# Group-wise modulation of the first norm in a diffusion layer, with the context rows prepared last

## The chip, the core and the metric

The kernel runs on one core of a Trainium2 chip. Its time is the device time of one launch in microseconds (us). "Before" is the median of three runs. The engines are TensorE (matmuls, PE in the profile; its weight loads are PEld), VectorE (DVE), ScalarE (ACT), GpSimd (POOL) and SyncE (SP), which issues nearly all DMA transfers here.

## What is computed

One layer of a diffusion transformer over 1024 latent tokens of 1024 features (x) with 256 context tokens (ctx), all in float32. What matters here is its beginning:

```python
sh1, sc1, g1, sh2, sc2, g2 = split(silu(c) @ w_mod + b_mod, 6)        # for the latents
csh1, csc1, ...            = split(silu(c_ctx) @ w_mod + b_mod, 6)    # for the context
h_lat = rms_norm(x, norm1_g) * (1 + sc1) + sh1
h_ctx = rms_norm(ctx, norm1_g) * (1 + csc1) + csh1
p_lat, p_ctx = h_lat @ w_in, h_ctx @ w_in      # columns: seven blocks of 512
```

`w_mod` is 1024 x 6144; the first norm uses its first 2048 columns, 1024 of shift and 1024 of scale. `w_in` is 1024 x 3584. Behind this stand retention and differential attention, an output projection and a gated MLP with a convolution; the change doesn't touch them.

## The kernel before

Features lie in 8 blocks of 128 (`KD` = 8, index `d` or `k`), latent tokens in 8 tiles of 128 (t = 0 to 7), context tokens in 2. A float32 product is made of three fast passes: each operand is split into a high part and a low part, and `passes` (L126) adds high x high, high x low and low x high (L129, L130, L131). The activations are kept transposed, features on partitions, as `hT[0]` (high) and `hT[1]` (low), each in two halves of 512 tokens; the context's are `cT`. A slice of `w_in` (two feature blocks of 512 columns, 512 KB, tile `raw`) is loaded and split into `whi` and `wlo` by `split_slice` (L181), four slices a block of columns; each call of `more` prepares one.

The first stage has these parts:

- `mod_part(i, q)` (L509) multiplies the two silu vectors (`cz`, padded to 32 columns for four strips of the array) with half of the rows of the i-th piece of `w_mod`, 512 columns wide. It loads two `wt` tiles of 512 KB, which share five buffers, and adds into the PSUM tile `pr`. Each call is four float32 matmuls, which the profile shows as eight. Between its loads the first four calls issue the load of one row tile of x (`xs`).
- `mod_columns(i)` (L522) copies `pr` to SBUF (`rw`, ScalarE), turns it into columns with four small matmuls (`pm`, eight in the profile) and adds the bias into `mcol` (VectorE; for a scale also the norm's gain).
- The four pieces come in the order scale of feature blocks 0 to 3, shift of 0 to 3, scale of 4 to 7, shift of 4 to 7; `lay_out` puts them so.
- `normalize` (L535) makes a row tile's sum of squares on ScalarE (`sq`), the reciprocal root on VectorE and GpSimd (`rsqrt`, L113) and the scaled rows on VectorE (L539).
- `modulate` (L541) does one feature block of up to four row tiles: TensorE transposes them into PSUM (`pt`, L545), ScalarE writes the high part (L548), VectorE the full value (`tmp`, L550), and VectorE or GpSimd, by turns, the low part (L552). `first_latents(half)` (L560) calls it for four blocks.
- `part_products(t, k)` (L564) adds feature block k's three passes into row tile t's PSUM tile `pn`, for column block 6 of `w_in`.

The order in the source (L590 to L627): pieces 0 and 1 with the first four row tiles, `first_latents(0)`, products of k = 0 to 3 for t = 0 to 3 with pieces 2 and 3 in between, `first_latents(1)`, products of k = 4 to 7 for t = 0 to 3. Beside these last run the steps of `other_rows` (L568): normalise the two context tiles and row tiles 4 to 7, modulate the context's eight blocks, then the latents' other eight. `beside(g, rate)` (L378) sets such a generator, and `tick` (L372), called after each product of three passes, takes `rate` steps of it on average; setting a new one first runs off the old one. Then come the context products of block 6 (L626), outside this scope row tiles 4 to 7 (L641), and the next stage, `transposed` with column block 5 (L644), whose PSUM tile is `pl`.

The source doesn't fix the engines' order. The framework schedules by its own estimates, with the source's order as priority, and so an engine's sequence in the trace can differ: the first product stands at 28.38 us on TensorE, and transposes of `first_latents(0)` that the source has ahead of it stand at 31.86 us. Within an engine's queue, and within SP's queue of DMA issues, the order is then fixed, and an instruction that waits holds those behind it.

## Time and profile before

| | us |
|---|---|
| median of three runs (lowest, highest) | 1414.38 (1412.52, 1414.53) |
| span of the profiled execution, first to last instruction | 1413.6 |
| first product `pn` starts | 28.38 |
| first `pl` starts (next stage) | 107.51 |
| TensorE busy | 1372.1 |
| VectorE / ScalarE / GpSimd busy | 991.1 / 729.1 / 286.1 |

The profile is of one execution, whose own time is known as its span, 1413.6 us. All times in the trace are counted from the span's start. Matmuls are pipelined and their ends are modelled, so two that follow each other overlap in the rows: what a matmul costs is read from one start to the next, not from its length. "Granted clock" is the share of full speed that TensorE's throttle gave. A wait is put down to what came last before the instruction started.

### The profile page before, as it was taken

Reading aid. Unit: us, or ns where it says so; the run is one execution under the profiler, and the core shown is the slowest. Engines: PE = TensorE matmul, PEld = TensorE weight load, DVE = VectorE, ACT = ScalarE, POOL = GpSimd, SP = SyncE. Lnnn points to the kernel's source line nnn. Section 1 sums busy time; section 2 is a strip of 40 time slices with the busy share of each in tenths; the row PEclk is TensorE's granted clock in tenths of the full one; section 3 lists DMA queues with packets and bytes.
Section 4 is the critical chain, followed back from the end, with each engine's and each line's share of the span. In section 5 each row is a group of like instructions: output and inputs, shape, how many; then the busy total and the mean of one; then the engine's idle time right before and its main releaser. Section 6 shows DMA issues by size and latency. Waiting matters only on the chain.

```text
span 1413.6 us, 19193 instructions
## 1 busy us (share of the span) xinstructions
PE 1372.1 (97%) x6924; PEld 1141.8 (81%) x6924; DVE 991.1 (70%) x1433; ACT 729.1 (52%) x1386; POOL 286.1 (20%) x321
## 2 busy tenths in 40 slices
PE   6999999999999999999999999999999999999996
PEld 2588888888888799998888778888888888888885
DVE  3464965334586798896357888877788777898457
ACT  3453312333565689997126645554455555455533
POOL 1220000000556133411201232233322220000001
PEclk8999999999999999999999999999999999999999
DMA  8645886365474796631421223223233226953224
GB/s 305 228 135 179 280 293 202 116 201 183 149 246 159 196 220 153 128 79 62 163 82 60 90 105 112 92 109 112 97 112 112 81 84 221 393 180 105 90 97 178
DMA packets 96662, 218.79 MB, mean 155 GB/s; under 512 B 9204, under 2 KB 31220, under 8 KB 96056
## 3 DMA queue, kind: packets, MB, share of 16 engines
q1 hardware_dynamic: 88408, 192.67, 39.3%
q0 software_dynamic: 8160, 24.91, 7.8%
q8 instruction: 54, 0.88, 0.2%
q14 instruction: 40, 0.33, 0.1%
HBM read 160.13 MB, written 57.41 MB: 154 GB/s over the span
## 4 chain that ended last, share of the span: by engine, by line
PE 81%; DMA 5%; issue 5%; DVE 4%; POOL 2%; ACT 2%; SPq 0%; POOLq 0%; DVEq 0%; ACTq 0%
PE pA L748 5%; PE pv L780 5%; PE chain L129 5%; PE chain L130 5%; PE chain L131 5%; PE c L131 4%; PE c L129 4%; PE c L130 4%; PE pn L130 3%; PE pn L129 3%; PE pn L131 3%; PE pl L129 3%; PE pl L131 3%; PE pl L130 3%; PE third L129 2%
## 5 line engine op out<-in xcount | busy, mean ns | idle before, releaser
L129 PE MATMUL chain<-T,whi 128*128 128x512 f32 x264 | 104.2, 395 | 4.7 <-ACT ua L1161 3.9
L129 PE MATMUL pl<-hT,whi 128*128 128x512 f32 x256 | 106.2, 415 | 0.0
L130 PE MATMUL chain<-T,whi 128*128 128x512 f32 x264 | 104.1, 394 | 0.0
L131 PE MATMUL chain<-T,wlo 128*128 128x512 f32 x264 | 103.9, 394 | 0.0
L131 PE MATMUL pl<-hT,wlo 128*128 128x512 f32 x256 | 100.2, 391 | 0.0
L130 PE MATMUL pl<-hT,whi 128*128 128x512 f32 x256 | 100.0, 391 | 0.0
L751 DVE TENSOR_REDUCE mt<-pA 128x1 f32<-128x1280 f32 x64 | 95.3, 1490 | 3.6 <-PE pA L748 2.1
L131 PE MATMUL c<-whi,ghl 128*128 128x512 f32 x232 | 90.4, 390 | 0.2 <-DVE ghl L1245 0.2
L748 PE MATMUL pA<-ks,qhl 128*128 128x512 f32 (+1 forms) x384 | 89.4, 369 | 1.0 <-ACT p L755 1.0
L130 PE MATMUL c<-wlo,ghl 128*128 128x512 f32 x232 | 90.3, 389 | 0.0
L129 PE MATMUL c<-whi,ghl 128*128 128x512 f32 x232 | 90.2, 389 | 0.0
L755 ACT ACTIVATE p<-pA,mt 128x1280 f32<-128x1280 f32 x64 | 85.5, 1337 | 6.7 <-DVE mt L751 4.5
L919 ACT CAST whi<-cmb 128x512 fp32r<-128x512 f32 x62 | 38.6, 623 | 86.4 <-PE chain L130 66.9
L129 PE MATMUL pn<-whi,hT 128*128 128x512 f32 x192 | 78.2, 408 | 0.0
L748 PEld LDWEIGHTS pA<-ks,qhl 128*128 128x128 f32 x384 | 67.6, 189 | 13.0 <-ACT p L755 1.4
L1074 POOL TENSOR_TENSOR cmb<-wrb 128x512 f32<-128x512 f32 x20 | 27.2, 1361 | 248.0 <-DMA wrb<-w_up 180.1
L780 PE MATMUL pv<-va,aT 128*128 128x128 f32 x640 | 77.0, 275 | 0.1
L130 PE MATMUL pn<-wlo,hT 128*128 128x512 f32 x192 | 76.1, 396 | 0.0
L131 PE MATMUL pn<-whi,hT 128*128 128x512 f32 x192 | 75.1, 394 | 0.5 <-DVE hT L552 0.5
L920 DVE TENSOR_TENSOR wlo<-cmb,whi 128x512 fp32r<-128x512 f32 x62 | 58.5, 946 | 23.1 <-ACT whi L919 23.1
L780 PEld LDWEIGHTS pv<-va,aT 128*128 128x128 f32 x640 | 74.0, 192 | 0.7 <-DVE yT L809 0.3
L115 POOL TENSOR_TENSOR sm<-sm,mhalf 128x1 f32<-128x1 f32 x26 | 16.1, 621 | 279.3 <-DVE sm L114 279.2
(302 smaller groups left out, 3809.3 us busy)
## 6 DMA issues: line engine op xcount, KB each, us to landing
wm<-w_mod SPq DMA_DIRECT2D x32, 512.0 KB, 5.4
raw<-w_in SPq DMA_DIRECT2D x28, 512.0 KB, 4.7
wra<-w_up SPq DMA_DIRECT2D x24, 512.0 KB, 3.3
wrb<-w_up SPq DMA_DIRECT2D x23, 512.0 KB, 3.5
W<-w_down SPq DMA_DIRECT2D x44, 256.0 KB, 6.0
ad<-s SPq DMA_DIRECT2D x20, 512.0 KB, 3.6
wra<-ad SPq DMA_DIRECT2D x20, 512.0 KB, 3.3
kvs<-kvg SPq DMA_DIRECT2D x36, 256.0 KB, 2.9
```

The lines of the kernel that those rows point to most:

```text
L115: nc.gpsimd.tensor_tensor(out=out_ap, in0=out_ap, in1=mhalf[:, :n], op=ALU.pow)
L129: mm(ps, lh, rh, start=first, stop=False, skip_group_check=more)
L130: mm(ps, lh, rl, start=False, stop=False, skip_group_check=more)
L131: mm(ps, ll, rh, start=False, stop=last, skip_group_check=more)
L748: mm(self.pa[m][:, c0:c1], self.q[:, m, i, qs], self.k[:, m, c0:c1], start=(i == 0), stop=(i == 1))
L751: nc.vector.tensor_reduce(out=self.mt[:, m : m + 1], in_=self.pa[m][:, :LK], axis=AX.X, op=ALU.min)
L755: nc.scalar.activation(self.p[m], self.pa[m][:, :LK], AF.Exp, scale=-1.0, bias=self.mt[:, m : m + 1], accum_out=self.s[:, m : m + 1])
L780: mm(self.pv, self.aT[:, c, :], self.v[:, c, :], start=(c == 0), stop=(c == NKT - 1))
L919: nc.scalar.copy(hi, src)
L920: nc.vector.tensor_tensor(out=lo, in0=src, in1=r32(hi), op=ALU.subtract)
L1074: nc.gpsimd.tensor_tensor(out=s1, in0=b1, in1=b2, op=ALU.add)
```

## The change

`w_mod`'s first 2048 columns are laid out in eight groups instead of four pieces: group d holds the 128 shift columns and the 128 scale columns of feature block d (1 MB, in two `wt` loads of 512 KB, again five buffers). `mod_load` issues a load, `mod_part(d, q)` does half of the rows with matmuls 256 wide, now in one PSUM tile with two halves that the groups use by turns, and `mod_columns(d)` turns one group with two small matmuls (four in the profile) and two VectorE operations. Products run over k with group k + 2's modulation between them, `latents(0, d)` modulates one block as soon as its group is there, and the loads of group k + 3 are issued ahead of products k.

The row loads of x are issued together at the start (three, then the fourth behind group 0's second half). Row tiles 4 to 7 get tiles of their own (`xs1`, no longer shared with `wt`), are loaded at k = 1 and 2, and are normalised and modulated by `second_rows` beside k = 5 to 7. The context rows come last: they are loaded at k = 6 into the `wt` buffers, prepared by `ctx_rows` beside the products of row tiles 4 and 5, and multiplied behind row tiles 6 and 7.

```diff
--- before.py
+++ after.py
@@ -506,31 +506,24 @@
             bsc = xp.tile([P, KD], F32, name="bsc", bufs=7)
             nc.vector.tensor_scalar(out=bsc, in0=cl[:, COL_BMOD + 8 : COL_BMOD + 16], scalar1=1.0, scalar2=None, op0=ALU.add)
 
-            def mod_part(i, q, between=None):
-
-                if q == 0:
-                    mods[i] = mm_tile("pr")
-                raw = []
-                for kk in (2 * q, 2 * q + 1):
-                    raw.append(xp.tile([P, 2, 512], F32, name="wt", tag="xt", bufs=5))
-                    nc.sync.dma_start(out=raw[-1], in_=w_mod[i][:, 2 * kk : 2 * kk + 2, :])
-                    if between is not None and kk % 2 == 0:
-                        between()
+            def mod_load(d, q):
+                wt = xp.tile([P, 4, 2 * P], F32, name="wt", bufs=5)
+                nc.sync.dma_start(out=wt, in_=w_mod[d][:, 4 * q : 4 * q + 4, :])
+                wts[d, q] = wt
+
+            def mod_part(d, q):
+                wt = wts.pop((d, q))
                 for g in range(4):
-                    mm(mods[i][32 * g : 32 * g + 32, :], cz[:, 4 * q + g, :], raw[g // 2][:, g % 2, :], start=(q == 0), stop=(q == 1))
-
-            def mod_columns(i):
-                d0, s = 4 * (i // 2), 1 - i % 2
-                rw = xp.tile([P, 512], F32, name="rw", bufs=2)
-                nc.scalar.copy(rw, mods[i])
-                pm = pst.tile([P, 4, 2], F32, name="pm", tag="tr")
-                for j in range(4):
+                    mm(mods[32 * g : 32 * g + 32, d % 2], cz[:, 4 * q + g, :], wt[:, g, :], start=(q == 0), stop=(q == 1))
+
+            def mod_columns(d):
+                rw = xp.tile([P, 2 * P], F32, name="rw", bufs=2)
+                nc.scalar.copy(rw, mods[:, d % 2])
+                pm = pst.tile([P, 2, 2], F32, name="pm", tag="tr")
+                for j in range(2):
                     mm(pm[:, j, :], rw[:, j * P : (j + 1) * P], fold, start=True, stop=True)
-                dst = mcol[:, d0 : d0 + 4, s, :]
-                bias = bsc[:, d0 : d0 + 4] if s else cl[:, COL_BMOD + d0 : COL_BMOD + d0 + 4]
-                nc.vector.tensor_tensor(out=dst, in0=pm, in1=bias.unsqueeze(2).to_broadcast([P, 4, 2]), op=ALU.add)
-                if s:
-                    nc.vector.tensor_tensor(out=dst, in0=dst, in1=cl[:, COL_N1 + d0 : COL_N1 + d0 + 4].unsqueeze(2).to_broadcast([P, 4, 2]), op=ALU.mult)
+                nc.vector.tensor_scalar(out=mcol[:, d, 1, :], in0=pm[:, 1, :], scalar1=bsc[:, d : d + 1], scalar2=cl[:, COL_N1 + d : COL_N1 + d + 1], op0=ALU.add, op1=ALU.mult)
+                nc.vector.tensor_scalar(out=mcol[:, d, 0, :], in0=pm[:, 0, :], scalar1=cl[:, COL_BMOD + d : COL_BMOD + d + 1], scalar2=None, op0=ALU.add)
 
             def normalize(xt, col):
                 sq = xp.tile([P, D], BF16, name="sq", bufs=1)
@@ -551,79 +544,93 @@
                 eng = nc.gpsimd if d % 2 else nc.vector
                 eng.tensor_tensor(out=lo, in0=tmp[:, :n], in1=r32(hi), op=ALU.subtract)
 
-            mods = {}
+            mods, wts = mm_tile("pr").rearrange("p (a b) -> p a b", a=2), {}
             wget, more = stream_parts(6)
+            xc = []
+            xs1 = [xp.tile([P, D], F32, name=f"xs1_{t}") for t in range(4)]
 
             def load_row(t):
-                nc.sync.dma_start(out=xs0[t], in_=x[t * P : (t + 1) * P, :])
-
-            def first_latents(half):
-                for d in range(4 * half, 4 * half + 4):
-                    modulate(xs0, d, 0, hT[0][0][:, d, :], hT[1][0][:, d, :])
+                nc.sync.dma_start(out=xs0[t] if t < 4 else xs1[t - 4], in_=x[t * P : (t + 1) * P, :])
+
+            def latents(half, d):
+                modulate((xs0, xs1)[half], d, 0, hT[0][half][:, d, :], hT[1][half][:, d, :])
 
             def part_products(t, k):
                 passes(part[t], lat_lhs(t, k), wget(k, 0, 512), k == 0, k == KD - 1)
                 tick()
 
-            def other_rows():
-                xc, xs = [], []
-                for t in range(NTC):
-                    xc.append(xp.tile([P, D], F32, name=f"xc{t}"))
-                    nc.sync.dma_start(out=xc[t], in_=ctxt[t * P : (t + 1) * P, :])
-                for t in range(4, 8):
-                    xs.append(xp.tile([P, D], F32, name="xt", tag="xt", bufs=5))
-                    nc.sync.dma_start(out=xs[-1], in_=x[t * P : (t + 1) * P, :])
+            def second_rows():
+                for t in range(4):
+                    normalize(xs1[t], 6 + t)
+                    yield
+                for d in range(KD):
+                    latents(1, d)
+                    yield
+
+            def ctx_rows():
                 for t in range(NTC):
                     normalize(xc[t], t)
-                    yield
-                for t in range(4, 8):
-                    normalize(xs[t - 4], 2 + t)
                     yield
                 for d in range(KD):
                     modulate(xc, d, 1, cT[0][:, d, :], cT[1][:, d, :])
                     yield
-                for d in range(KD):
-                    modulate(xs, d, 0, hT[0][1][:, d, :], hT[1][1][:, d, :])
-                    yield
 
             store = store_to(dv_row, c0=NTC)
-            for i in range(2):
-                for q in range(2):
-                    t = 2 * i + q
-                    mod_part(i, q, lambda: load_row(t))
-                    normalize(xs0[t], 2 + t)
-                    if i:
-                        more()
-                mod_columns(i)
-            mod_part(2, 0)
-            first_latents(0)
+            mod_load(0, 0)
+            for t in range(3):
+                load_row(t)
+            mod_load(0, 1)
+            load_row(3)
+            more()
+            for n in range(2, 5):
+                mod_load(*divmod(n, 2))
+            for q in range(2):
+                mod_part(0, q)
+            mod_load(2, 1)
+            for t in range(4):
+                normalize(xs0[t], 2 + t)
+            mod_columns(0)
+            latents(0, 0)
+            for q in range(2):
+                mod_part(1, q)
+            mod_columns(1)
+            latents(0, 1)
+            more()
             part = [mm_tile("pn") for _ in range(4)]
-            for k in range(4):
-                for t in range(4):
-                    part_products(t, k)
-                if k == 0:
-                    mod_part(2, 1)
-                    mod_columns(2)
-                if k == 1:
-                    mod_part(3, 0)
-                if k == 2:
-                    mod_part(3, 1)
-                    mod_columns(3)
-            more()
-            more()
-            first_latents(1)
-            first.close()
-            cp = pctx.enter_context(tc.tile_pool(name="cp", bufs=1, side="right"))
-            cT.extend(cp.tile([P, KD, LC], F32R, name=f"cT{a}") for a in range(2))
-            beside(other_rows(), 0.9, 0.0)
-            for ts in ((0, 1), (2,), (3,)):
-                for k in range(4, KD):
-                    for t in ts:
-                        part_products(t, k)
-                for t in ts:
-                    store(t, part[t])
-            side["rate"] = 0.6
-            natural(wget, ctx_lhs, range(NTC), store_to(dv_row))
+            for k in range(KD):
+                n = k + 2
+                if k == 5:
+                    beside(second_rows(), 0.9)
+                if k == 6:
+                    first.close()
+                    cp = pctx.enter_context(tc.tile_pool(name="cp", bufs=1, side="right"))
+                    cT.extend(cp.tile([P, KD, LC], F32R, name=f"cT{a}") for a in range(2))
+                    for t in range(NTC):
+                        xc.append(xp.tile([P, D], F32, name="xc", tag="wt", bufs=5))
+                        nc.sync.dma_start(out=xc[t], in_=ctxt[t * P : (t + 1) * P, :])
+                if n + 1 < KD:
+                    for q in range(2):
+                        mod_load(n + 1, q)
+                if k in (1, 2):
+                    load_row(2 * k + 2)
+                    load_row(2 * k + 3)
+                if k in (1, 3):
+                    more()
+                part_products(0, k)
+                if n < KD:
+                    mod_part(n, 0)
+                part_products(1, k)
+                if n < KD:
+                    mod_part(n, 1)
+                part_products(2, k)
+                if n < KD:
+                    mod_columns(n)
+                    latents(0, n)
+                part_products(3, k)
+            for t in range(4):
+                store(t, part[t])
+            beside(ctx_rows(), 0.7)
+            natural(wget, lat_lhs, range(4, 6), store)
             beside(iter(()), 0.0)
         rc = late.enter_context(tc.tile_pool(name="rc", bufs=1))
         gn = rc.tile([P, 2, 512], F32, name="gn")
@@ -638,7 +645,8 @@
         m2p = m2c.enter_context(tc.tile_pool(name="m2p", bufs=1))
         pad(m2p, 128)
         rtab = load_rope(1)
-        natural(wget, lat_lhs, range(4, NT), store)
+        natural(wget, lat_lhs, range(6, NT), store)
+        natural(wget, ctx_lhs, range(NTC), store_to(dv_row))
         wg = stream_block(5)
         beside(modulations2(), 37 / 156)
         transposed(wg, dk_d, rtab, 32, 1.0, LC, by_head[:1])
@@ -1420,7 +1428,7 @@
         "rows": rows,
         "consts": consts,
         "rope": rope,
-        "w_mod": kmajor(a["w_mod"][0][:, : 2 * D], 4)[[2, 0, 3, 1]],
+        "w_mod": kmajor(a["w_mod"][0][:, : 2 * D].reshape(D, 2, KD, P).transpose(0, 2, 1, 3).reshape(D, 2 * D), KD),
         "w_mod2": a["w_mod"][0][:, 2 * D :].reshape(KD, P, 4, D).transpose(2, 0, 1, 3),
         "w_in": w_in,
         "w_out": kmajor(a["w_out"][0], 2),
```

## The prediction

> **What bounds the kernel now.** I read the page first, for the bound of the whole.
>
> ```profile
> PE 1372.1 (97%) x6924; PEld 1141.8 (81%) x6924; DVE 991.1 (70%) x1433; ACT 729.1 (52%) x1386; POOL 286.1 (20%) x321
> ```
>
> TensorE is busy for 97% of the span, so time is only to be had where it idles or runs slowly. The view of busy time by stretch says where. Its columns are the stretch, its length, each engine's busy time (and instructions), the granted clock, the DMA share and GB/s.
>
> ```profile
> 0.00:28.30 28.30, 16.27 (x59) 6.46 (x60) 6.86 (x24) 9.55 (x15) 2.73 (x9) 0.87 0.93 359
> 28.30:35.00 6.70, 6.70 (x26) 3.39 (x25) 5.06 (x7) 2.60 (x4) 2.04 (x2) 0.78 0.27 84
> 35.00:51.90 16.90, 16.90 (x84) 9.73 (x84) 2.72 (x5) 3.07 (x4) 0.89 (x1) 1.00 0.92 329
> 51.90:70.40 18.50, 15.00 (x74) 10.85 (x73) 12.80 (x25) 14.07 (x26) 8.50 (x10) 1.00 0.37 133
> 70.40:107.50 37.10, 36.96 (x180) 30.41 (x179) 25.61 (x63) 22.16 (x48) 9.15 (x9) 1.00 0.42 139
> 107.50:1413.60 1306.10, 1280.30 (x6509) 1080.95 (x6507) 938.04 (x1313) 677.63 (x1291) 262.80 (x292) 0.99 0.46 149
> ```
>
> Until 28.3 us DMA is saturated (share 0.93) and TensorE has little to do; from 28.3 to 51.9 it is always busy, and at 0.78 clock in the first 6.7 us; from 51.9 to 70.4 it idles for 18.5 - 15.0 = 3.5 us; from 70.4 on it is full. The change lies before 107.5, where the next stage (`pl`) begins, and touches none of the 1306 us behind it.
>
> The timeline shows what the first 28 us wait for. In brackets stands the idle time before an instruction and what ended it.
>
> ```profile
> 5.82 1.92 PE L520 MATMUL pr<-wt,cz 128*32 128x512 f32 x4 [5.82 <-DMA wt<-w_mod]
> 6.99 1.06 ACT L537 ACTIVATE sq<-xs 128x1024 bf16<-128x1024 f32 x1 [3.86 <-DMA xs<-x]
> ...
> 12.85 0.19 PEld L520 LDWEIGHTS pr<-wt,cz 128*32 128x32 f32 x4 [2.36 <-DMA wt<-w_mod]
> ...
> 20.33 1.06 ACT L537 ACTIVATE sq<-xs 128x1024 bf16<-128x1024 f32 x1 [1.46 <-DMA xs<-x]
> ...
> 21.60 0.19 PEld L520 LDWEIGHTS pr<-wt,cz 128*32 128x32 f32 x4 [2.41 <-DMA wt<-w_mod]
> ...
> 22.33 0.75 DVE L539 TENSOR_SCALAR xs<-xs,sm 128x1024 f32<-128x1024 f32 x1 [0.66 <-POOL sm L115]
> ```
>
> The timeline of TensorE alone goes on from there:
>
> ```profile
> 25.93 2.80 PE L545 MATMUL pt<-ident,xs 128*128 128x128 f32 x12
> 28.38 0.78 PE L129 MATMUL pn<-whi,hT 128*128 128x512 f32 x1
> 28.96 0.63 PE L130 MATMUL pn<-wlo,hT 128*128 128x512 f32 x1
> 29.38 0.63 PE L129 MATMUL pn<-whi,hT 128*128 128x512 f32 x1
> ```
>
> Read the first fence as a ladder: the 512 KB transfers land in the order of their issue, whether they carry w_mod, rows or w_in: the first at 5.82, the second at 6.99, the sixth (wt, row, wt, wt, row, wt) at 12.85, the thirteenth at 21.60, that is 8.75 us / 7 = 1.25 us each. The first product (`pn`, 28.38) needs the whole shift block of the first four feature blocks, which ends with the thirteenth transfer. Products then start 0.42 us apart (28.96 to 29.38), against 0.23 later: the half clock.
>
> **The change part by part.**
>
> *First product.* Group 0 now needs only two `wt` transfers, besides the four rows. By the new order of issue (wt, three rows, wt, row, raw) the last row is the sixth transfer: 12.85. From the arrival of the last row to its scaled form took 20.33 to 22.33 + 0.75, that is 2.75 us: 15.6. From the first transpose to the first product took 25.93 to 28.38, that is 2.45 us, half clock included: **18.05 instead of 28.38, -10.3 us**. At best the eight transposes of the next blocks go behind it (eight of twelve in 2.45 us, 1.6 us fewer): 16.4. At worst the cast of the first `w_in` slice (`raw`, seventh transfer, 14.1; its cast is as long as `sq`, about 1.05) is queued ahead of the last row's square: the square starts at 15.1 instead of 12.85, 20.3 in all. I take 18.05, since the same instructions followed one another so in the trace.
>
> *Work on TensorE behind the first product.* The prices are start-to-start. A product takes 0.23, so two products without an insert take 0.45:
>
> ```profile
> 107.28 0.39 PE L131 MATMUL pn<-whi,hT 128*128 128x512 f32 x1
> 107.51 0.39 PE L129 MATMUL pl<-hT,whi 128*128 128x512 f32 x1
> ```
>
> An insert of 4 modulation matmuls, 512 wide, costs 36.92 - 35.28 - 0.45 = 1.19 us, and one of 8 no more, 47.84 - 46.18 - 0.45 = 1.21:
>
> ```profile
> 35.28 0.39 PE L129 MATMUL pn<-whi,hT 128*128 128x512 f32 x1
> 35.60 1.05 PE L520 MATMUL pr<-wt,cz 128*32 128x512 f32 x4
> 36.59 0.50 PE L130 MATMUL pn<-wlo,hT 128*128 128x512 f32 x1
> 36.92 0.39 PE L131 MATMUL pn<-whi,hT 128*128 128x512 f32 x1
> ```
> ```profile
> 46.18 0.39 PE L131 MATMUL pn<-whi,hT 128*128 128x512 f32 x1
> 46.50 1.07 PE L520 MATMUL pr<-wt,cz 128*32 128x512 f32 x8
> 47.50 0.50 PE L129 MATMUL pn<-whi,hT 128*128 128x512 f32 x1
> 47.84 0.39 PE L130 MATMUL pn<-wlo,hT 128*128 128x512 f32 x1
> ```
>
> In the same way 8 `pm` cost 40.62 - 39.26 - 0.45 = 0.91:
>
> ```profile
> 39.26 0.40 PE L130 MATMUL pn<-wlo,hT 128*128 128x512 f32 x1
> 39.49 0.95 PE L528 MATMUL pm<-fold,rw 128*128 128x2 f32 x8
> 40.30 0.47 PE L131 MATMUL pn<-whi,hT 128*128 128x512 f32 x1
> 40.62 0.39 PE L129 MATMUL pn<-whi,hT 128*128 128x512 f32 x1
> ```
>
> Twelve transposes at half clock took 2.45 us (25.93 to 28.38); four at full clock are put at half of a third, 0.41.
>
> - `mod_part`: before, 4 calls (32 matmuls) stood behind the first product, broken into 7 inserts (six of 4 matmuls, one of 8): 7 x 1.2 = 8.4. After, 6 groups x 2 calls = 12 inserts of 8 matmuls of 256. That width isn't in the trace: between half of the 1.00 us that the 512-wide ones took (46.50 to 47.50) and the whole of it. I take half, since half as many columns are streamed, and a little for what doesn't shrink; the switch of 0.2 us stays: 12 x 0.75 = 9.0. **+0.6** (at most +6.1).
> - `pm`: before, 2 inserts of 8, 1.8. After, 6 inserts of 4, each half of 0.91 or at most the whole; half and a bit for the switch, 0.5: 3.0. **+1.2** (at most +3.6).
> - Transposes: before, 12 of the 80 lay ahead of the first product; after, 8 (`d` 0 and 1). One more four: **+0.4**.
>
> The 240 products and their order inside a tile cost the same. Moving the context products behind `natural` of tiles 6 and 7 moves as many matmuls. The half-clock start is there in both.
>
> *The idle 3.5 us (51.9 to 70.4).* They go as they stand: context rows are no longer wanted in the middle but after 96 further products. **-3.5.** What is late next is the second half of x: four normalisations and eight modulations, fed in from `k` = 5 on, then wanted by tile 4 at once. The stretch above shows such a load: VectorE 12.8 and ScalarE 14.1 us in 18.5, beside 15 us of TensorE work. The new stretch has about as much of either beside 36 products (8.2), two `mod_part` (1.5), one `pm` (0.5) and ten times four transposes (4.1), 14.3 us of it. So I put a new wait between 0 and the same 3.5: **+2.0**.
>
> *Waits that the groups add.* Each group is a chain: `mod_part`, ScalarE's copy `rw`, `pm`, the two VectorE operations into `mcol`, then `latents`. `pm` waits for `rw`; behind it in TensorE's queue stand that group's transposes and the next products.
>
> ```profile
> PE pm L528 <- ACT rw L525: 1.4, 2, 0.7
> ```
>
> Before, two of four waited, 0.7 us each, both before products stood beside them; the other two did not. Six new ones: 0 to 4.2, **+1.5**. VectorE's two short operations a group lie beside products of the group before; if that cover is gone, they are part of rival 1.
>
> *The DMA queue.* SP is moved past nothing that it waited for, but every `wt` load waits for a slot (five) that only `mod_part` frees. In the trace DMA falls to 84 GB/s from 28.3 to 35.0 for that, since `mod_part` stood behind other work. After, 28 transfers at 1.25 us from 5.82 would land the last `wt` at about 40 us; its `mod_part` comes at `k` = 5, about 18 + 5 x 5.1 = 44 us (a group is 2.7 + 1.5 + 0.5 + 0.4). The margin is 1.5 to 2 us at group 2 (tenth and eleventh transfer, 17.9 and 19.1, behind the first and second tile's products) and grows, so I cost this at nothing. If that cover is gone, each late load is a wait of 1.25 us or more.
>
> **Sum**: -10.3 + 0.6 + 1.2 + 0.4 - 3.5 + 2.0 + 1.5 = -8.1 us on the profiled 1413.6, so 1405.5. The runs' median (1414.4) is 0.8 above that span: **1406.3 us**. One cost at a time at its end gives -9.8 (the best start), -9.6 (no wait for `rw`), -10.1 (no wait for the rows), -5.8 (the late start), -5.4 (every `rw`) and -2.6 (full-price inserts); best ends together give -13. This case's own range is 1401.5 to 1412.
>
> At one place the Trainium skill speaks against the change. In the trace the granted clock is 0.87 and 0.78 in the two stretches in and behind the waits for DMA and 1.00 where TensorE is dense. "TensorE: Matmul & The Clock Gate", section "Loop structure matters more than you think", says that a loop which waits for a DMA before each burst of matmuls drops the array to half clock each time. The trace agrees for the start; whether the new groups are such a loop is the second rival.
>
> **The rivals.**
> 1. *The group's chain becomes the bound.* Products of `k` wait for `latents(k)`, two groups ahead in the source. For it: the engines' order is not the source's (at 28.38 a product runs ahead of other transposes), so the lead may shrink to one group, and VectorE and GpSimd share the low halves. Against it: at 40 to 47 us the same chain cost products nothing. Price: 0.7 us for `rw` and as much again for `mcol` and `hT`, six times, is 8 us instead of 1.5, less if the rows' wait goes into it: -8.1 + 6.5 = -1.6, 1412.8; with half of it 1409.5.
> 2. *Slower: the loads come late and the clock falls.* If `mod_part` stands late in TensorE's order, its slot is freed late, the next load lands late, and each group waits. Six waits of one rung (1.25) are 7.5. At half clock the 12 products of a group cost 12 x (0.42 - 0.23) = 2.3 more and its inserts about as much, 4 x 6 = 24 if every group is hit. Half of that: -8.1 + 7.5 + 12 = +11.4, 1426. It decides from the point where waits and half clock eat 8.1 us, 1.3 us a group, which is one late rung in each. For it: the 84 GB/s of that stretch. Against: the margin above at every group.
> 3. *The earlier start isn't taken.* The first product is queued behind group 1's transposes and both raw casts: about 21 us, and the mid-stage wait stays whole: -7.3 + 2.2 - 3.5 + 3.5 + 1.5 = -3.6, 1410.8. A changed order of instructions behind 107.5 could give or take a little more.
>
> **How the numbers follow.** Forecast 0.64 (all of it faster by over 0.2%, 2.8 us, about what a measurement of this kernel can tell from no change); rival 1 0.14 (0.07 faster, 0.06 same, 0.01 slower); rival 2 0.12 (slower); rival 3 0.10 (0.05 faster, 0.03 same, 0.02 slower). So faster 0.76, same 0.09, slower 0.15. The range for 8 in 10 goes from 1401.5 to 1416: it leaves out most of rival 2 and a little at the low end.
>
> **What would show it.** First `pn` near 18 us instead of 28.4; first `pl` near 99.5 instead of 107.5; inserts of `mod_part` near 0.75; less than 2 us idle around the row change; no `pr` waiting for `wt` after 18 us; the stage behind `pl` still 1306 us long. I am wrong if `pl` starts later than 107, if the clock is under 0.9 between 25 and 50 us, or if the stage behind `pl` changes its length.

## The result, and the profile after

| | before | after |
|---|---|---|
| median of ten runs (lowest, highest), us | 1415.82 (1412.52, 1418.85) | 1413.24 (1411.45, 1416.94) |
| ratio after / before | | 0.9986 [0.9973, 0.9999] |
| span of the profiled execution | 1413.6 | 1409.6 |
| first product `pn` | 28.38 | 17.77 |
| first `pl` (next stage) | 107.51 | 103.83 |
| from there to the end of the span | 1306.1 | 1305.8 |

The forecast was 8.1 us less; 2.6 us less came, inside what was to be called no change. The profiled pair differs by 4.0 us; of the changed kernel it was the fastest of ten runs (1411.45 us) that was profiled. The start of the products moved as forecast, by 10.6 us, but the next stage starts only 3.7 us earlier: 7 us of lead were lost between 17.8 and 103.8 us. The stage behind didn't change.

The page of the changed kernel, its first line and the busy times:

```profile
span 1409.6 us, 19335 instructions
...
PE 1365.5 (97%) x6988; PEld 1139.6 (81%) x6988; DVE 991.9 (70%) x1443; ACT 729.8 (52%) x1390; POOL 286.9 (20%) x321
```

There are 64 matmuls more than before (6988 against 6924): a float32 matmul counts twice in the record, and 256 columns instead of 512 take twice as many. Its busy time by stretch (same columns as in the prediction):

```profile
0.00:17.70 17.70, 5.26 (x32) 2.17 (x32) 5.99 (x22) 8.09 (x13) 2.73 (x9) 1.00 0.89 325
17.70:23.40 5.70, 5.70 (x32) 3.52 (x31) 1.89 (x4) 0.37 (x1) 0.00 (x0) 1.00 0.92 362
23.40:41.00 17.60, 17.14 (x115) 10.99 (x115) 7.65 (x17) 8.20 (x13) 4.11 (x4) 1.00 0.93 356
41.00:60.00 19.00, 17.32 (x118) 10.72 (x117) 9.41 (x19) 8.76 (x15) 2.89 (x4) 1.00 0.60 210
60.00:77.00 17.00, 14.29 (x73) 10.32 (x73) 13.76 (x19) 11.21 (x19) 8.98 (x7) 1.00 0.26 94
77.00:103.80 26.80, 26.80 (x123) 22.10 (x122) 14.70 (x53) 15.31 (x40) 4.43 (x6) 1.00 0.42 158
```

Before, TensorE was always busy from the first product on, but for 3.5 us between 51.9 and 70.4; now it has small holes everywhere between 23 and 77 us: 0.5 + 1.7 + 2.7 us. What ended them is in the view of waits, from the first product to the next stage (us in total, times, longest):

```profile
PE pt L538 <- DVE tmp L543: 2.3, 3, 0.8
PE pn L129 <- ACT hT L541: 1.0, 2, 0.6
PE pn L131 <- POOL hT L545: 0.6, 3, 0.2
PE pn L130 <- DVE wlo L187: 0.4, 1, 0.4
PE pn L129 <- ACT whi L186: 0.3, 1, 0.3
```

No load of w_mod is waited for, no wait is longer than 0.9 us; it is the engines that feed TensorE, a little at a time. And the timeline of TensorE shows how fast the first products run:

```profile
16.35 0.48 PE L538 MATMUL pt<-ident,xs 128*128 128x128 f32 x1 [1.24 <-DVE xs L532]
16.76 1.08 PE L517 MATMUL pr<-wt,cz 128*32 128x256 f32 x8
17.77 0.80 PE L129 MATMUL pn<-whi,hT 128*128 128x512 f32 x1
18.37 0.63 PE L130 MATMUL pn<-wlo,hT 128*128 128x512 f32 x1
18.79 0.63 PE L129 MATMUL pn<-whi,hT 128*128 128x512 f32 x1
...
23.36 0.64 PE L517 MATMUL pr<-wt,cz 128*32 128x256 f32 x8
23.93 0.50 PE L131 MATMUL pn<-whi,hT 128*128 128x512 f32 x1
24.26 0.39 PE L129 MATMUL pn<-whi,hT 128*128 128x512 f32 x1
24.49 0.40 PE L130 MATMUL pn<-wlo,hT 128*128 128x512 f32 x1
```

Products stand 0.42 us apart at 18.37 and 0.23 at 24.26; the insert of eight takes 1.01 us (16.76 to 17.77) and then 0.57 (23.36 to 23.93). That is half clock until about 22 us, though the column of the granted clock says 1.00 for 17.7 to 23.4: the column knows no more than the events that the record has, and the first in this one, at 22.1 us, is the rise to full clock.

For the rest a table is of more use than rows. It adds up TensorE's timeline from the first product to the first `pl`, one start to the next, without the idle times over 0.15 us, which stand apart; split behind the 24th product, about where the clock is up. "Again" is another profiled execution of the same kernel (first experiment).

| us | start | products 1 to 24 | 25 to `pl` | of it products (216) | `pr` | `pm` | `pt` | idle | `pl` |
|---|---|---|---|---|---|---|---|---|---|
| before | 28.38 | 14.01 | 65.12 | 52.68 | 1.98 | 0.81 | 6.15 | 3.50 | 107.51 |
| before again | 25.90 | 12.74 | 65.76 | 53.44 | 1.98 | 0.81 | 6.36 | 3.17 | 104.40 |
| after | 17.77 | 12.74 | 73.31 | 54.74 | 5.26 | 1.91 | 6.83 | 4.57 | 103.83 |
| after again | 18.51 | 12.89 | 73.34 | 54.75 | 5.26 | 1.92 | 6.83 | 4.57 | 104.74 |

So the loss is in the second stretch, about 8 us longer after the change; and the old kernel differs from itself by 3.1 us at `pl`.

### The profile page after: what moved, and what is told of

The parts are those of the page before. It is cut to its first block, busy times and chain, and to the rows that moved or that the text cites. A ratio compares the mean times of both kernels' runs of the same rounds, so it can differ in the third digit from the quotient of the medians.

```text
span 1409.6 us, 19335 instructions
## 1 busy us (share of the span) xinstructions
PE 1365.5 (97%) x6988; PEld 1139.6 (81%) x6988; DVE 991.9 (70%) x1443; ACT 729.8 (52%) x1390; POOL 286.9 (20%) x321
## 4 chain that ended last, share of the span: by engine, by line
PE 79%; DMA 6%; issue 5%; DVE 5%; POOL 3%; ACT 2%; SPq 0%; POOLq 0%; DVEq 0%; ACTq 0%
PE chain L129 5%; PE pA L756 5%; PE chain L130 5%; PE pv L788 5%; PE chain L131 5%; PE c L131 4%; PE c L130 4%; PE c L129 4%; PE pn L130 4%; PE pn L131 3%; PE pn L129 3%; PE pl L131 3%; PE pl L129 3%; PE pl L130 3%; DMA W<-w_down 2%
## 5 line engine op out<-in xcount | busy, mean ns | idle before, releaser
L129 PE MATMUL chain<-T,whi 128*128 128x512 f32 x264 | 103.8, 394 | 5.0 <-ACT ua L1169 3.9
```

Of the source, the lines that this page charges most:

```text
L129: mm(ps, lh, rh, start=first, stop=False, skip_group_check=more)
```

## The experiments

Times of one batch share the runs of the kernel before; ratios are to that. The start of the next stage (`pl`) is exact within one execution and says what the front did; the whole time has 2 us of scatter of its own.

### Both kernels again, and each half of the change alone

Two theories stand against each other. The prediction's own, from its parts: groups and moved context each bring some us. The rival, from the trace after: the groups alone make the difference, the idle time in the middle only changes its cause.

`e0_before_again` and `e1_after_again` are the two kernels unchanged.

> The kernel before, unchanged, for a second profile. If the single profile can be trusted for the first stage, the first product starts at 28.4 and pl at 107.5, each within 0.3 us, and what differs from run to run lies behind pl (1306.1 us in the first profile). If the first stage itself varies, pl moves by 1 us or more and a difference of 4 us between two profiles says little.

> The changed kernel, unchanged, for a second profile. By the first profile the first product starts at 17.8 and pl at 103.8. If that repeats within 0.3 us, the first stage is 3.7 us shorter for certain, and the stretch behind pl (1305.8 us in the first profile) is what makes the medians of ten runs differ by only 2.6.

`e2_context_last` is the old order of modulation with the context last (its loads behind the second rows'):

```diff
-            side["rate"] = 0.6
-            natural(wget, ctx_lhs, range(NTC), store_to(dv_row))
+            beside(ctx_rows(), 0.7)
+            natural(wget, lat_lhs, range(4, 6), store)
...
-        natural(wget, lat_lhs, range(4, NT), store)
+        natural(wget, lat_lhs, range(6, NT), store)
+        natural(wget, ctx_lhs, range(NTC), store_to(dv_row))
```

> The kernel before with only the context rows moved last: four modulation pieces as before, row tiles 4 to 7 prepared beside k = 4 to 7, context beside row tiles 4 and 5 and multiplied behind 6 and 7. Theory A: the idle time in the middle belongs to VectorE's and GpSimd's load and only changes its cause, so pl stays at 107 (106.5 to 107.5) and the time within 0.1%. Theory B, the prediction's: the 3.5 us of idle time go and at most 2 come back, so pl is at 105.5 to 104.

`e3_groups_alone` is the changed kernel with the context rows where they were (loaded and prepared from k = 5 on, ahead of the second rows):

```diff
-            beside(ctx_rows(), 0.7)
-            natural(wget, lat_lhs, range(4, 6), store)
+            side["rate"] = 0.6
+            natural(wget, ctx_lhs, range(NTC), store_to(dv_row))
```

> The changed kernel with the context rows back in the middle: eight groups, then context rows and row tiles 4 to 7 prepared in the old order, context products ahead of row tiles 4 to 7. Theory A: the groups alone make the difference, pl at 103 to 105. Theory B: without the context moved last the old 3.5 us of idle time come on top, pl at 106 to 108, and the time is that of before.

Measured (before in this batch: 1415.02, 35 runs from 1409.96 to 1420.13):

| | median, us | ratio | start | `pl` | idle before `pl` |
|---|---|---|---|---|---|
| before again | 1414.39 | 0.9993 [0.9982, 1.0004] | 25.90 | 104.40 | 3.2 |
| after again | 1413.24 | 0.9993 [0.9979, 1.0007] | 18.51 | 104.74 | 4.7 |
| context last alone | 1417.45 | 1.0019 [1.0007, 1.0030] | 27.68 | 108.13 | 4.5 |
| groups alone | 1413.41 | 0.9995 [0.9984, 1.0007] | 17.68 | 103.78 | 4.2 |

The groups alone do what the whole change does. The context alone brings nothing (it is even slower), and the hole that it was to close gets larger. (Its front ran at half clock, as in the first profile of before, so its `pl` is to be compared with 107.51.) The first two of five rows of its view of waits, from 30 us to the next stage:

```profile
PE pt L545 <- DVE tmp L550: 2.5, 3, 1.0
PE pt L545 <- DVE sm L114: 0.9, 2, 0.6
```

The second rows' transposes now wait for VectorE as the context's had before. The prediction's theory fell here, the rival held.

These runs also show why the old kernel's front varies. Its busy times by stretch in the execution on which the prediction rested:

```profile
20.00:25.00 5.00, 2.81 (x10) 0.98 (x8) 1.03 (x3) 1.74 (x3) 0.55 (x1) 0.60 1.03 420
25.00:30.00 5.00, 5.00 (x22) 4.71 (x22) 2.26 (x4) 2.94 (x4) 0.00 (x0) 0.50 0.58 238
```

and in the other execution of the same kernel:

```profile
15.00:20.00 5.00, 4.39 (x18) 1.00 (x17) 2.16 (x5) 2.19 (x3) 0.55 (x1) 0.66 1.03 420
20.00:25.00 5.00, 2.94 (x20) 1.67 (x19) 1.39 (x4) 1.74 (x3) 0.55 (x1) 1.00 1.03 420
25.00:30.00 5.00, 5.00 (x27) 2.35 (x25) 4.08 (x5) 3.84 (x5) 0.65 (x1) 1.00 0.70 254
```

The clock fell in both in the stretch where TensorE waits for loads; in the first it was down just when the transposes and first products came, in the second it was up again by then. Its timeline there, against 2.45 us and 0.42 in the prediction:

```profile
24.39 1.51 PE L545 MATMUL pt<-ident,xs 128*128 128x128 f32 x12
25.90 0.50 PE L129 MATMUL pn<-whi,hT 128*128 128x512 f32 x1
26.23 0.39 PE L130 MATMUL pn<-wlo,hT 128*128 128x512 f32 x1
26.46 0.39 PE L129 MATMUL pn<-whi,hT 128*128 128x512 f32 x1
```

### Is TensorE's own work what sets the pace?

`e4_insert_twice` multiplies the first half of groups 2 to 7 twice, into the same place:

```diff
             def mod_part(d, q):
                 wt = wts.pop((d, q))
+                for g in range(4) if q == 0 and d > 1 else ():
+                    mm(mods[32 * g : 32 * g + 32, d % 2], cz[:, 4 * q + g, :], wt[:, g, :], start=True, stop=True)
```

> The changed kernel, where the first half of groups 2 to 7 is multiplied twice (the same four matmuls issued again into the same place): 48 more matmuls of 256 columns in the record, in six inserts twice as long. Theory 'TensorE's own work sets the pace between the first pn and pl': each costs what 8 such matmuls took, 0.55 to 0.78 us, so the first pl moves from 103.8 to 104.7 to about 107 to 109.4, idle time before it unchanged at 4 to 5 us. Rival 'the chain rw, pm, mcol, hT or the feeding engines set the pace' : the first pl moves by less than 1.5 us and the idle time falls by 2 to 4 us.

Measured: `pl` at 102.44, 1.4 us earlier than the changed kernel, with 48 matmuls (2.7 us of `pr`) more; one run, 1412.22. TensorE's idle time is down from 4.6 to 2.1, and of the waits two kinds are left that matter:

```profile
PE pt L540 <- DVE tmp L545: 1.2, 2, 1.0
PE pn L131 <- POOL hT L547: 0.7, 3, 0.4
```

So the theory that TensorE's work alone sets the pace fell: the idle time is 2.5 us less, about what the added work takes. But this run also has another order: the framework plans with its own estimates, and with longer inserts it put products and transposes elsewhere (216 later products 53.91 us instead of 54.74, for one). How much of the idle time the added work filled and how much the order took away can't be told apart here.

### The half clock

Matmuls that nobody reads keep the array busy while it waits. `e5_warm`, on the changed kernel, and `e7_before_warm`, on the old one:

```diff
+            warm = pst.tile([P, 2 * P], F32, name="warm", tag="tr")
+            def turn_over(n, src):
+                for _ in range(n):
+                    mm(warm, ident, src[:, : 2 * P], start=True, stop=True)
...
                 mod_part(0, q)
+                if q == 0:
+                    turn_over(10, cl)
...
             mod_columns(0)
+            turn_over(3, xs0[2])
             latents(0, 0)
```

```diff
                     normalize(xs0[t], 2 + t)
+                    if (i, q) in ((0, 1), (1, 0)):
+                        for _ in range(4):
+                            mm(warm, ident, xs0[t][:, : 2 * P], start=True, stop=True)
```

> The changed kernel, with 13 float32 matmuls of 256 columns added whose product nobody reads: ten behind group 0's second half, which are to run while TensorE waits for loads and rows, and three ahead of group 0's transposes. Theory 'half clock': the change left TensorE so sparse at the start that the first products (17.8 to about 23.4 us) run at half speed, 0.42 apart instead of 0.23. With the array kept busy, products stand 0.23 apart from the first one on, the first pn starts at 17 to 18 us, the first pl at 101 to 101.5 instead of 103.8 to 104.7, and the time is 2 to 3 us under the changed kernel's: ratio to before 0.996 to 0.998. Rival 'behind the products the engines that feed them are the bound' (VectorE's backlog between 60 and 77 us, the casts of w_in): products start faster and wait longer; TensorE's idle time before pl grows from 4.6 us to 6.5 or more, the first pl stays at 103 or later, and the ratio stays at 0.9985 to 1.0.

> The kernel before, with eight such idle matmuls added, four behind piece 0's second half and four behind piece 1's first half, while TensorE waits for loads. Theory 'half clock': the kernel before differs from execution to execution (first pl at 104.4 or at 107.5 to 108.1) because the array sometimes falls to half clock between 18 and 26 us and sometimes not. Kept busy there it doesn't fall: first pn at 25.5 to 28.4, first products 0.23 apart, first pl at 104.4 or less, time up to 3 us under before, ratio 0.998 to 1.0, and the spread of the runs smaller than the 4 to 10 us of before. Rival 'the 3 us are something else' (a late transfer, another order): products 0.42 apart again at 26 to 32 us in spite of the work, or 0.23 apart and yet a first pl at 107.

| | median, us | ratio | start | products 1 to 24 | 25 to `pl` | `pl` |
|---|---|---|---|---|---|---|
| `e5_warm` | 1415.39 | 1.0004 [0.9991, 1.0017] | 18.98 | 10.82 | 73.33 | 103.13 |
| `e7_before_warm` | 1413.73 | 0.9991 [0.9978, 1.0003] | 24.92 | 12.75 | 65.76 | 103.43 |

The old kernel with eight idle matmuls starts its next stage earlier than the changed kernel does, and its time can't be told from the changed kernel's. In `e5_warm` products are 0.23 apart from the first, but the start came 1.2 us late:

```profile
14.39 0.70 PE L591 MATMUL warm<-xs,ident 128*128 128x256 f32 x2 [1.38 <-DVE xs L532]
14.93 0.50 PE L524 MATMUL pm<-fold,rw 128*128 128x2 f32 x4
...
17.05 1.06 PE L538 MATMUL pt<-ident,xs 128*128 128x128 f32 x4
```

An idle matmul stood ahead of `pm` and waited for the third row (1.38 us); on VectorE the last row's root and scale stand behind the `mcol` that needs `pm`. `e13_warm2` therefore takes `cl` and the copy `rw` as sources, so that nothing waits:

```diff
+            turn_over(10, cl)
             for q in range(2):
                 mod_part(0, q)
...
             mod_columns(0)
+            turn_over(4, rws[0])
             latents(0, 0)
```

> The changed kernel with the idle matmuls placed so that nothing waits behind them: ten on the constants ahead of group 0, four on the copy rw behind group 0's pm. The earlier version kept the clock but held pm back by 1 us, with it VectorE's mcol and the last row's scale behind it. Theory 'half clock': first pn at 17.3 to 18.0, products 0.23 apart from there, TensorE's time from the first pn to the first pl without idle 79.5 instead of 81.5, pl at 101.3 to 102.3. Rival 'feeders': what the clock gives is lost again in waits for hT and tmp (idle 6 or more), pl at 103 or later.

Its timeline:

```profile
13.12 3.00 PE L592 MATMUL warm<-rw,ident 128*128 128x256 f32 x8
15.91 1.06 PE L539 MATMUL pt<-ident,xs 128*128 128x128 f32 x4
16.90 0.82 PE L517 MATMUL pr<-wt,cz 128*32 128x256 f32 x8
17.84 0.50 PE L129 MATMUL pn<-whi,hT 128*128 128x512 f32 x1
18.18 0.40 PE L130 MATMUL pn<-wlo,hT 128*128 128x512 f32 x1
18.42 0.40 PE L129 MATMUL pn<-whi,hT 128*128 128x512 f32 x1
```

Start 17.84, products 0.24 apart, products 1 to 24 in 10.85 us instead of 12.74, `pl` at 102.01: the clock theory held for the front, 1.9 us. But the idle matmuls did not hold the clock all the time. It was up from 7.1 us, fell again and came back just ahead of the first product, so that the insert at 16.90 still took 0.94 us (columns as above; TensorE was busy for all 3.40 us at a granted clock of 0.50):

```profile
13.90:17.30 3.40, 3.40 (x14) 2.32 (x16) 2.04 (x3) 1.46 (x4) 0.55 (x1) 0.50 1.02 419
```

In `e5_warm` it was down from 15.4 to 18.8, and up again for its first product at 18.98. That neither start fell into such a stretch is in part luck.

The stretch from product 25 on took 73.32, as in the changed kernel. But the time didn't follow: 1415.32, ratio 1.0000 [0.9991, 1.0009]. Behind `pl` this execution took 1311.8 us instead of 1305.8, and TensorE's instructions there are the same in the same order. Set side by side instruction by instruction, 2.4 of these 6.0 us are lost between 300 and 500 us, where the changed kernel's own second profile loses 2.2 too; 1.5 between 730 and 745 us, which only the three kernels that add idle matmuls to the changed one lose (1.3 to 1.6); and 1.6 between 800 and 850 us, where the clock fell to half for 3.4 us twice in this profile, once in the changed kernel's first and never in its second.

The tail lies between 1305.3 and 1311.8 us in the sixteen profiles of this study. The three kernels with idle matmuls on the changed one have 1309.3, 1310.7 and 1311.8, but without any `e2_context_last` has 1309.9 and `e15_early_slices` and `e11_half_loads` 1309.5, so the idle matmuls can't be called the cause of the whole. Among the twelve profiles of the changed kernel and its variants, the three with `pl` at 103.78 or later have tails of 1305.5 to 1306.2, the nine with an earlier `pl` 1307.7 to 1311.8: part of what a front wins is lost again behind it. Why is not settled.

### VectorE's backlog between 60 and 77 us

`e9_spread` spreads the context's ten steps over four row tiles, `e10_warm_spread` is that with the idle matmuls of `e13_warm2`:

```diff
-            beside(ctx_rows(), 0.7)
-            natural(wget, lat_lhs, range(4, 6), store)
+            beside(ctx_rows(), 0.35)
+            natural(wget, lat_lhs, range(4, NT), store)
```

> The changed kernel, with the context rows' ten steps spread over row tiles 4 to 7 at a rate of 0.35 instead of over tiles 4 and 5 at 0.7. Theory 'VectorE's backlog': between 60 and 77 us VectorE has the second rows' and the context rows' steps on top of one another (13.8 of 17 us busy) and TensorE's transposes wait for it. Spread out, VectorE's busy time there falls to 12 or less, the waits of 64 to 76 us (2.3 us) fall under 1, idle time before pl goes from 4.6 to about 2.5, and pl starts at 101.5 to 102.5 instead of 103.8 to 104.7. Rival 'the second rows alone make the waits': the wait for tmp stays at 2 us or more and pl at 103.3 or later. On the whole time 2 us are a ratio 0.0015 lower than the change's.

> Both edits, idle matmuls and spread context rows. If the two losses are independent, pl at 99.5 to 100.5 (both gains of about 2 us), and the time about 4 us under the changed kernel's, ratio to before 0.996. If they share one cause (the feeding engines), pl no earlier than the better of the two alone less 1 us.

| | median, us | ratio | start | products 1 to 24 | 25 to `pl` | `pl` |
|---|---|---|---|---|---|---|
| `e9_spread` | 1412.25 | 0.9988 [0.9979, 0.9997] | 17.73 | 11.74 | 73.11 | 102.58 |
| `e10_warm_spread` | 1413.64 | 0.9995 [0.9983, 1.0006] | 17.10 | 10.86 | 73.17 | 101.13 |

VectorE has less to do there, as planned:

```profile
60.00:77.00 17.00, 14.44 (x72) 10.58 (x71) 12.59 (x16) 8.91 (x16) 7.61 (x6) 1.00 0.30 107
```

(12.59 instead of 13.76), and the wait for `tmp` falls from 2.3 to 1.4, but the idle time stays 4.5 to 4.7. From the 96th product to the 144th it wins 1.5 us (16.4 instead of 17.9), from there to the 192nd, where the context's steps now stand, it gives 1.3 back. Of the 1.25 us that `pl` gained in `e9_spread`, 1.0 lies in the first 24 products, an earlier end of the half clock, by chance. The backlog theory fell: the work was moved, not hidden.

### Loads

`e11_half_loads` leaves out the loads of the second half of w_mod in groups 3 to 7 and multiplies the first half twice there:

```diff
-                    for q in range(2):
-                        mod_load(n + 1, q)
+                    mod_load(n + 1, 0)
...
-                wt = wts.pop((d, q))
+                wt = wts.pop((d, q)) if q == 0 or d < 3 else last[0]
+                last[:] = [wt]
```

> The changed kernel without the loads of the second half of w_mod in groups 3 to 7; the first half is multiplied there twice (so the modulation of five blocks leaves out half of w_mod's rows). As many matmuls, five transfers of 512 KB fewer, 6.25 us of DMA by 1.25 each. Theory 'loads pace the middle': DMA is full from 30 to 41 us (share 1.01), so w_in's slices and the second rows come late, and TensorE waits 2.0 us between 40 and 55 for casts and hT. With fewer loads that idle time goes and pl starts at 101.5 to 102.5. Rival 'the engines' own chains': the idle time of 40 to 55 us stays (1.5 or more) and pl moves by less than 0.8.

Measured: 1407.15, ratio 0.9950 [0.9938, 0.9963], `pl` at 97.12: three times what the load theory had expected. The stretch from product 25 on took 66.99 us, with every term smaller (products 53.27, `pr` 4.14, `pt` 5.99, idle 1.77). But it isn't the same program otherwise: the framework made another order with it, with the inserts of `pr` in 9 places instead of 13. So loads and order had to be told apart.

SyncE's queue in the changed kernel (each row a group of issues) stands on four `wt` loads from 12.9 to 24.4 us, waiting for one of five buffers, with second rows and w_in's third slice behind them:

```profile
12.93 11.45 SPq L511 DMA_DIRECT2D wt<-w_mod  x4
24.43 0.90 SPq L553 DMA_DIRECT2D xs<-x  x2
25.43 0.38 SPq L183 DMA_DIRECT2D raw<-w_in  x1
```

`e14_six` has six buffers (and one `rw` for two), in the same order of instructions on every engine:

```diff
-                wt = xp.tile([P, 4, 2 * P], F32, name="wt", bufs=5)
+                wt = xp.tile([P, 4, 2 * P], F32, name="wt", bufs=6)
```

`e15_early_slices` issues slices and rows ahead of the group's `wt` loads, and `e16_six_early_spread` takes both and the spread context:

```diff
+                if k in (0, 2):
+                    more()
+                if k in (1, 2):
+                    load_row(2 * k + 2)
+                    load_row(2 * k + 3)
                 if n + 1 < KD:
                     for q in range(2):
                         mod_load(n + 1, q)
-                if k in (1, 2):
-                    load_row(2 * k + 2)
-                    load_row(2 * k + 3)
-                if k in (1, 3):
-                    more()
```

> The changed kernel with six wt buffers instead of five (rw has one instead of two, to make room). SyncE's queue stands from 12.9 to 24.4 us on four wt loads that wait for a buffer; the second rows (24.4) and w_in's third slice (25.4) are queued behind them, and DMA falls from 423 to 109 GB/s between 21 and 27 us. Theory 'loads wait for buffers, and what is queued behind them comes late': with a sixth buffer the row loads are issued 1 to 3 us earlier, TensorE's idle time between 40 and 55 us falls from 1.9 to under 1, pl starts 1 to 2 us before 103.8 to 104.7. Rival 'loads are not the cause': the row loads are issued earlier and pl moves by less than 0.5 us.

> The changed kernel, with w_in's third and fourth slice and the second rows issued ahead of the wt loads of the same group instead of behind them; nothing is left out. Theory 'queued behind': the third slice is issued at about 12 us instead of 25.4 and the fourth at under 30 instead of 34.7, their casts come earlier, the waits of products for casts, hT and whi between 40 and 55 us (1.9 us) go to under 1, and pl starts at 102.3 to 103.3. Against it stands that the wt loads then come one transfer (1.25 us) later: if the groups' loads are what paces the products, TensorE waits for wt behind 18 us and pl is at 104 or later.

> Six buffers, early slices and the context rows spread over row tiles 4 to 7, together: the version that the runs so far point to. If the three losses are separate, pl at 100.5 to 101.5 and the time 3 us under the changed kernel's, ratio to before 0.9965. If the half clock at the start and the number of inserts are all that is left, idle time before pl stays at 3 or more and the ratio at 0.998 to 0.999, as with the spread alone.

| | median, us | ratio | start | products 1 to 24 | 25 to `pl` | `pl` |
|---|---|---|---|---|---|---|
| `e14_six` | 1414.34 | 0.9996 [0.9983, 1.0009] | 18.06 | 12.03 | 73.35 | 103.44 |
| `e15_early_slices` | 1414.21 | 0.9997 [0.9984, 1.0009] | 17.93 | 11.84 | 72.42 | 102.19 |
| `e16_six_early_spread` | 1412.98 | 0.9990 [0.9977, 1.0004] | 17.55 | 10.87 | 72.79 | 101.20 |

With six buffers the queue moves on 2.7 us earlier:

```profile
12.13 9.52 SPq L511 DMA_DIRECT2D wt<-w_mod  x4
21.70 0.90 SPq L553 DMA_DIRECT2D xs<-x  x2
22.70 0.38 SPq L183 DMA_DIRECT2D raw<-w_in  x1
```

and TensorE's waits are the same as in the changed kernel, row for row; of its view of waits the first and the last:

```profile
PE pt L538 <- DVE tmp L543: 2.3, 3, 0.9
...
PE pn L129 <- ACT whi L186: 0.3, 1, 0.3
```

In this order, then, the standing queue is not what TensorE waits for; six buffers leave the amount that is loaded as it was. Earlier slices win 0.9 us in the second stretch with another order, and no time that can be measured. All three together have the earliest `pl` but one of the kernels that compute everything, but most of that lies in the first 24 products (10.87 us instead of 12.74), where order and the end of the half clock both changed, and the ratio is no better than the changed kernel's own. That `e11_half_loads` was so much faster may be its order or the 2.5 MB that it doesn't load; the two could not be told apart, since every version with its loads put back got another order. No kernel that computes everything beats the changed one by more than the scatter.

## Why the prediction was wrong, step by step

Against the profiled execution of before, each step and what the profile after has for it:

| step of the prediction | forecast, us | measured, us |
|---|---|---|
| first product | -10.3 | -10.6 |
| `mod_part` behind it | +0.6 | +0.8 |
| `pm` | +1.2 | +1.0 |
| transposes | +0.4 | +1.0 |
| "the 240 products ... cost the same" | 0 | +3.1 |
| idle time: -3.5, +2.0, +1.5 | 0 | +1.1 |
| behind `pl` | 0 | -0.3 |
| sum | -8.1 | -4.0 |

(Each is the sum of both stretches: products 63.08 instead of 60.02, for one; the measured terms make -3.9, the rest is rounding.)

Of the 4.1 us by which the pair falls short of the sum, then, 3.1 are the products, 1.1 the idle time and 0.6 the transposes; the other terms give about 0.6 back.

- **First product: right in total** for the execution at hand (17.77 for 18.05), but by two errors that nearly cancel: the last row was scaled at 16.29 instead of 15.6, since its square started at 13.21 instead of 12.85 and its root stood behind `mcol` on VectorE; and from there to the first product it took 1.48 us instead of 2.45, since one transpose and ScalarE's `hT` were left to do, not twelve transposes. And its 28.38 wasn't the kernel's but that execution's: with the clock up the old kernel starts at 25.90, kept up at 24.92. Against those the gain is 8.1 or 7.1 us.
- **Inserts: right in price.** Between 29.06 and 30.29 an insert of eight 256-wide matmuls costs 1.23 - 0.45 = 0.78 us (forecast 0.75):

```profile
29.06 0.40 PE L129 MATMUL pn<-whi,hT 128*128 128x512 f32 x1
29.38 0.64 PE L517 MATMUL pr<-wt,cz 128*32 128x256 f32 x8
29.95 0.50 PE L130 MATMUL pn<-wlo,hT 128*128 128x512 f32 x1
30.29 0.39 PE L131 MATMUL pn<-whi,hT 128*128 128x512 f32 x1
```

  Wrong in number: group 1's second half, its `pm` and its transposes came to stand behind the first product (13 inserts, 28 `pm` and 76 transposes, not 12, 24 and 72). An earlier start had been counted as a gain, and work that was then still to do not as its price.
- **The step that failed: "the 240 products and their order inside a tile cost the same" and "the half-clock start is there in both".** Products cost 3.1 us more. 1.0 us lies in the first 24 (8.34 instead of 7.33), which the idle matmuls show to be clock: 6.74 in `e13_warm2`. In both profiles of the changed kernel the first products run at half clock; in the old kernel's only in one of two. The other 2.1 us lie in the later 216, and their cause is worked out, not tested. There 51 products stand next to something else instead of 41, and one of those takes 0.31 us and one between products 0.23, which gives 0.8; the rest is that their mean rose from 0.30 to 0.32 us, waits under 0.15 us among it.
- **Idle time: wrong cause, nearly the right size.** It didn't go, neither with the context moved alone (4.5 us) nor with the change. The second rows' wait was forecast at 2.0; transposes wait 2.3 for VectorE, 1.4 of it the second rows' (64.97 and 68.71) and 0.85 the context's own (72.99). The chains of the groups were put at 1.5 and are 2.3, with the casts of w_in, which the prediction hadn't named. Of rival 1, the chain as the bound, this may be a mild form: with more work in `e4_insert_twice` `pl` came no later.
- **The DMA queue at nothing: right.** No `pr` waits for `wt` behind the first product, and loads issued 2.7 us earlier change no wait.
- **Rival 2, the clock falling in each group: wrong** beyond the start. Every hole is under 0.9 us, and the granted clock is 1.00 in each stretch from 23.4 us to the next stage. The Trainium skill, "TensorE: Matmul & The Clock Gate", section "Part 1: The HAM clock gate (the "warmup" mystery)", says that the array's default is the throttled state and that about 3.4 us of sustained work release it. The trace agrees with the first part, half clock at the start; for the second it has more, about 6 us from 16.35, where the work of the changed kernel becomes dense, to full speed at 22; in `e9_spread`, with the same order there, it was under 4 us, from 16.32 to about 20.
- **Profile against median.** The sum was made against one execution, and a bad one in its front. Two profiles of the old kernel differ by 3.1 us at `pl`, one has the changed kernel's 103.83 behind it by 3.7 us, the other by 0.6. The medians, 2.6 us apart in one batch and 1.8 in the other, lie between. The profiled execution of the changed kernel took 1411.45 us, 1.8 less than the median of its ten, so the pair's 4.0 us overstate the change.

What stays open: why the kernels with an earlier `pl` are longer behind it, and how much of `e11_half_loads` is order and how much loads.

## What to carry to other kernels

An earlier start of a bound engine is worth only what isn't merely moved behind it: count all its work from the new start to a fixed point behind the change, not the start alone, and price the breaks that finer interleaving puts between its instructions. Where the clock depends on what ran before, look whether the changed front still raises it, and take two executions of the kernel before as the base, for one may owe some us to its clock. When a hole has a feeding engine at its end, moving one of its jobs away lets the next one end it. And an earlier start of the next stage is not yet an earlier end: here wins of up to 2.7 us at `pl` didn't show in the whole time.

## What the runs showed of the hardware

- In the changed kernel's profile the array runs at half speed at the start while the column of the granted clock says 1.00: eight 256-wide matmuls took 1.01 us at 16.76 and 0.57 at 23.36, both under 1.00.
- From product 25 to `pl` the time is repeated to 0.04 us (73.31 to 73.35) in the five profiles that share the changed kernel's order there, with idle matmuls and six buffers too, while the first varies by 2 us with the clock.
- Two long instructions of VectorE lost time beside GpSimd: in the changed kernel's timeline below, the scale of a row takes 1.79 us and the split of a slice of w_in 2.31, against 0.75 and 1.22 where GpSimd has nothing to do (15.54 and 16.21). Each is 1.0 to 1.1 us longer, and each starts while GpSimd is at a low half of 1.68 us (from 65.71 and 69.46) and runs beside it for 1.24 us. Not every overlap costs: VectorE's own low half at 65.55, begun before GpSimd's at 65.71, took its usual 0.68. No run took GpSimd's work away, so the cause is read from the rows.

```profile
66.15 1.79 DVE L532 TENSOR_SCALAR xc<-xc,sm 128x1024 f32<-128x1024 f32 x1
...
69.90 2.31 DVE L187 TENSOR_TENSOR wlo<-raw,whi 128x1024 fp32r<-128x1024 f32 x1
```
